# Which PSUM banks, which free places and which first products: one change to a two-layer decoder trunk in fp32

## The chip, the cores and the metric

The kernel runs on one core of a Trainium2 chip. The metric is device time in microseconds (us) of one execution; lower is better. The kernel before was timed in three runs: 577.90, 578.51 and 579.87 us, median 578.51.

## The reference

The input is x, 256 tokens by 1024, in float32. Two layers follow, each a token mixer and a gated MLP, and after each of these four parts x becomes LayerNorm(alpha * x + part).

- Layer 0 mixes with a gMLP: z = gelu(x @ w_in) (1024 by 2048) is halved into u and v, v is normalised, each of 8 groups of 128 channels is mixed over positions by a causal 128 by 128 matrix (once for each of two chunks of 128 tokens), a bias is added, and (u * mixed) @ w_out follows.
- Layer 1 mixes with attention: qkv = x @ w_qkv, 16 heads of 64. With 256 tokens there is one block, so it is plain causal attention with a relative position bias, and then @ w_o.
- The MLP: h = x @ w_up (1024 by 5632), a causal convolution of width 3 over tokens, gelu(g) * val, @ w_down (2816 by 1024).

## The kernel before

**Products in halves.** Every large product of fp32 matrices is made of three TensorE products of rounded parts: a matrix is split into `hi` (rounded to fp32r by ScalarE or VectorE) and `lo` (the rest, a VectorE subtraction, line 344), and hi*hi + hi*lo + lo*hi is summed in PSUM. `split` (line 357) records both instructions. All TensorE products of this kind have line 326 in the profile, all transposes line 332.

**Weights.** They come from HBM in 76 chunks of 1 MB in the order of `stream`. `prep(i)` (line 385) loads chunk i into one of two `raw` buffers and splits it into two pairs `whi`, `wlo` of 128 by 1024. Five chunks (`CHUNKS`) are prepared at the start; `spent` prepares chunk i + 5 when chunk i has been used. The first two chunks are loaded and split in pieces (`FIRST`, line 382). x comes transposed (`xT`) in four pieces (`XFIRST`), each split by `load_xt` (line 433), with its tiles in the order token half, k tile. The rank in these tables is the order of the loads on SP's queue. With two `raw` buffers, chunk 2 waits for the splits of chunk 0, chunk 3 for those of chunk 1.

**PSUM.** Eight banks (lines 271 to 316): four tiles of one bank each (`bank0` to `bank3`, the list `ALONE`), and two tiles of two banks each (`twos0`, `twos1`), whose halves can also be handed out one by one: banks 4 and 6 are the halves of `twos0`, 5 and 7 those of `twos1`, and `couple(j)` names such a pair. `bank()` hands out the oldest free single bank, or a half if all four are held long; `half()` a half of the tile that was used least recently; `taken(i, long)` a given one.

**Order.** Each helper records an operation with an estimated time in a plan. `Plan.emit` (line 122) walks through the plan with these estimates, gives every operation a due time from those that need it, and writes the instructions in the order of its own start times. TensorE's main products keep the recorded order; operations with `fill=True` (position mixing, scores, transposes, application of the attention weights) are put between them as soon as the plan finds them ready. On the chip each engine works through its instructions in that order, and waits where something is not ready. The plan knows of a PSUM half only by its own last user; the waits on the chip are put in by the framework from the accesses to the tiles in the written order.

**The stages.** `gmlp` (line 639): v by rows into four single banks (96 products of 512 columns, for k tiles 0 to 3 both token halves in turn, then each half alone); then eight groups of column products for u (`cols_times`, 24 products of 256 columns each, line 678: into a half), each read by ScalarE's gelu, with `spatial(g)` (line 667, also into a half) for the group three before. `project_out` (line 583) multiplies by w_out, w_down or w_o into four long held single banks and, for the last token half, two halves (`ends`), adds the residual and normalises. `conv_up` is the first half of the MLP. `moba` (line 758) is attention: V by rows into the four halves (line 771, token half 0 into couple 0), then for eight pairs of heads `project` (q, then k; line 787, into a half), `scores` (line 805, two single banks), `softmax`, `turn` (line 838, one single bank and three transposes for each head) and `apply` (line 849).

Of the kernel before, what the change touches and what calls it, by code (L numbers as in the profile page):

```python
# [11 lines left out]
F32 = mybir.dt.float32  # L12
# [6 lines left out]
P = 128  # L19
D = 1024  # L20
S = 256
DEPTH = 2
KT = D // P
FFN = 2816
FT = FFN // P
NT = S // P
# [9 lines left out]
HALF = 512  # L36
CH = 2048
# [8 lines left out]
T1_WAITS = (2600, 3300, 4000, 4700)  # L46
REST = 25000
AHEAD = 12000


class Buf:
# [172 lines left out]
def trunk_kernel(ctx: ExitStack, tc: tile.TileContext, a: dict, out: bass.AP):  # L224
# [64 lines left out]
    def couple(j):  # L289
        return j + BANKS // 2, j + BANKS // 2 + len(twos)  # L290
# [62 lines left out]
    def load(o, src, w, r=(), nbytes=None, rank=None):  # L353
        nbytes = nbytes or flat(o) * P * 4
        plan.op("sp", nbytes / 360.0, lambda: nc.sync.dma_start(o, src), r, w, nbytes=nbytes, rank=rank)  # L355
# [24 lines left out]


    FIRST = {0: [(0, 512, 0), (512, 1024, 2), (1024, 2048, 4)], 1: [(0, 1024, 6), (1024, 2048, 7)]}
    XFIRST = ((0, 1, 1), (1, 1, 3), (2, 2, 5), (4, 4, 8))

    def prep(i):
        name, c = stream[i]
        raw = raws.new()
        cuts = FIRST.get(i, [(0, CH, None)])
        for s, e, rank in cuts:
            load(raw.ap[:, s:e], a[name][c, :, s:e], [(raw, range(s // 256, e // 256))], rank=rank)  # L390
        subs = []
        for s in range(2):
            hi, lo = whi.new(), wlo.new()
            pieces = [(0, 512), (512, 1024)] if i in FIRST or i in FINE else [(0, SUB)]
            for b, e in pieces:
                src = raw.ap[:, s * SUB + b:s * SUB + e]
                split((hi, range(b // 256, e // 256), hi.ap[:, b:e]), (lo, range(b // 256, e // 256), lo.ap[:, b:e]),
                      (raw, range((s * SUB + b) // 256, (s * SUB + e) // 256), src))
            subs.append((hi, lo))
        chunks[i] = subs  # L400
# [5 lines left out]
    def sub(name, c, s):  # L406
        return chunks[where[name, c]][s]
# [18 lines left out]
    def xt_view(b):  # L426
        return b.ap

    xh, xl = xt_new()
    xT32 = place("ff", HALF, KT * S)  # L430
    xv32 = xT32.ap.rearrange("p (t k c) -> p t k c", t=NT, k=KT)

    def load_xt(k, n, rank):
        load(xv32[:, :, k:k + n, :], a["xT"][:, :, k:k + n, :], [(xT32, [(t, j) for t in range(NT) for j in range(k, k + n)])],
             rank=rank)
        for t in range(NT):
            parts = [(t, j) for j in range(k, k + n)]
            split((xh, parts, xt_view(xh)[:, t, k:k + n, :]), (xl, parts, xt_view(xl)[:, t, k:k + n, :]),
                  (xT32, parts, xv32[:, t, k:k + n, :]), by="dve" if k == 0 else "act")

    prep(0)
    for k, n, rank in XFIRST:
        load_xt(k, n, rank)
    for i in range(1, CHUNKS):
        prep(i)
    xtok = [Buf(t) for t in xs_]
# [192 lines left out]
    def gmlp():  # L639
        at = xt_at(xh, xl)  # L640
        pieces = [[(o, HALF, bank(True)) for o in (0, HALF)] for _ in range(NT)]
        order = [(k, t) for k in range(4) for t in range(NT)] + [(k, t) for t in range(NT) for k in range(4, KT)]
        v = []
        for k, t in order:
            rows_step(pieces[t], *at(k, t), *sub("a_v", k // 2, k % 2), k == 0, k == KT - 1)
            if t == NT - 1 and k % 2:
                spent("a_v", k // 2)
            if (k, t) == (3, NT - 1):
                rows = ln_rows(0)
                ws, bs = load_mixer()  # L650
            if k == KT - 1:
                vt = place("ff", HALF + t * D, D)
                for o, n, b in pieces[t]:
                    act(vt.ap[:, o:o + n], b.ap, AF.Gelu_apprx_tanh, [b], [(vt, range(o // S, (o + n) // S))],
                        psum=True, table="gelu")
                    done_with(b)
                st, mean, rstd = stats(vt, vt.ap, [(0, HALF), (HALF, HALF)])
                scaled(vt, vt.ap, st, mean, rstd, rows)
                v.append(vt)
        load_rest()  # L660
        mh, ml = place("rr", 0, KT * S), place("rr", KT * S, KT * S)
        hv, lv = (b.ap.rearrange("p (k s) -> p k s", k=KT) for b in (mh, ml))
        uring = Places("ff", [0, S, HALF + 2 * D, HALF + 2 * D + S], S)
        yring = Places("ff", range(5120, 6144, S), S)
        us = {}

        def spatial(g):
            b, y = half(), yring.new()
            mms([(b.ap[:, c * P:(c + 1) * P], v[c].ap[:, g * P:(g + 1) * P], ws[1][:, g, :], True, True)
                 for c in range(NT)], [(v[c], [g // 2]) for c in range(NT)] + [ws[0]], [b], fill=True)  # L670
            y3 = y.ap.rearrange("p (c t) -> p c t", c=NT)
            tt(y3, b.ap[:, :S].rearrange("p (c t) -> p c t", c=NT), bs[1][:, g:g + 1, :].to_broadcast([P, NT, P]),
               ALU.add, [b, bs[0]], [y])
            tt(y.ap, y.ap, us[g].ap, ALU.mult, [y, us[g]], [y])
            split((mh, [g], hv[:, g, :]), (ml, [g], lv[:, g, :]), (y, [0], y.ap))

        for g in range(GROUPS):
            b = half()
            cols_times(b, xh, xl, *sub("a_u", g // 2, g % 2))
            if g % 2:  # L680
                spent("a_u", g // 2)
            us[g] = uring.new()
            act(us[g].ap, b.ap[:, :S], AF.Gelu_apprx_tanh, [b], [us[g]], psum=True, table="gelu")
            if g >= 3:
                spatial(g - 3)
        for g in range(GROUPS - 3, GROUPS):
            plan.later(600 * (g - GROUPS + 4), lambda g=g: spatial(g))
        return lambda k, t: (hv[:, k, t * P:(t + 1) * P], lv[:, k, t * P:(t + 1) * P], [(mh, [k]), (ml, [k])])
# [69 lines left out]
    def moba(h, l, scr):  # L758
# [9 lines left out]
        ohv, olv = (b.ap.rearrange("p (k s) -> p k s", k=KT) for b in (oh, ol))  # L768
        vhv, vlv = (b.ap.rearrange("p (t d) -> p t d", t=NT) for b in (vh, vl))
        at = xt_at(h, l)  # L770
        pieces = [[(o, HALF, taken(i, True)) for o, i in zip((0, HALF), couple(j))] for j in range(NT)]
        for ks in (range(5), range(5, KT)):
            for t in range(NT):
                for k in ks:
# [10 lines left out]
        held, biases = {}, {}  # L785

        def project(i, j):
            b, t = half(), qkring[j].new()
            cols_times(b, h, l, *sub("b_qk", i, j))

            n, at2, scale = (P, P, DH ** -0.5) if j == 0 else (S, 0, 1.0)
            src, (th, tl) = b.ap[:, at2:at2 + n], (x.new() for x in qkparts[j])
            act(t.ap, b.ap[:, :P], AF.Copy, [b], [t], scale=scale, psum=True)
            act(th.ap, src, AF.Copy, [b], [th], scale=scale, psum=True)
            stt(tl.ap, src, scale, th.ap.bitcast(F32), ALU.mult, ALU.subtract, [b, th], [tl])
            t = (t, th, tl)
            held.setdefault(i, []).append(t)
            if j == 0:
                biases[i] = bring.new()
                load(biases[i].ap, bass.AP(tensor=scr.ap.tensor, offset=scr.ap.offset + 2 * i * DIST,  # L800
                                           ap=[[1, P], [DIST, 2], [1, S]]), [biases[i]], [scr])
            else:
                spent("b_qk", i)

        def scores(i):
            ((q0, qh, ql), (k0, kh, kl)), bias = held[i], biases[i]
            bank2 = [bank() for _ in range(2)]


            def both(o, seq):  # L810
                return [(bank2[hh].ap[:, o[0]:o[1]], x.ap[hh * DH:(hh + 1) * DH], y.ap[hh * DH:(hh + 1) * DH],
                         n == 0, n == len(seq) - 1) for n, (x, y) in enumerate(seq) for hh in range(2)]

            mms(both((0, P), [(q0, k0)]) + both((P, P + S), [(qh, kh), (qh, kl), (ql, kh)]),
                [q0, qh, ql, k0, kh, kl], bank2, fill=True)
            held[i] = [softmax(bank2[hh], bias, hh) for hh in range(2)]
# [20 lines left out]

        def turn(i):
            ph, pl = (x.new() for x in pring)
            for hh in range(2):  # L840
                e, b = held[i][hh], bank()

                transposes([(b.ap[:, c * P:(c + 1) * P], e.ap[:, c * P:(c + 1) * P]) for c in range(3)],
                           [(e, [0, 1])], [b])
                sl = slice(hh * (P + S), (hh + 1) * (P + S))
                split((ph, [hh], ph.ap[:, sl]), (pl, [hh], pl.ap[:, sl]), (b, [0], b.ap[:, :P + S]), psum=True)
            held[i] = ph, pl
# [57 lines left out]
def _layout(i):  # L905
# [10 lines left out]
    def paired(wa, wb):  # L916
# [3 lines left out]
    w_in, qkv = np.asarray(i["a_w_in"])[0], np.asarray(i["b_w_qkv"])[0]  # L920
    g = {
        "x": f(x.reshape(NT, P, D).transpose(1, 0, 2)),
        "xT": f(x.reshape(NT, P, KT, P).transpose(3, 0, 2, 1)),
        "a_v": by_rows(w_in[:, D:]),
        "a_u": f(tiles(w_in[:, :D]).reshape(4, 2, P, SUB).transpose(0, 2, 1, 3).reshape(4, P, CH)),
        "a_out": by_rows(np.asarray(i["a_w_out"])[0]),
# [45 lines left out]
```

## Time and profile before

| what | value |
|---|---|
| median of three runs | 578.51 us (577.90 to 579.87) |
| the profiled execution, its own time | 579.16 us |
| its span, first to last instruction | 577.5 us |
| TensorE (PE) busy | 560.1 us, 97% of the span |
| VectorE (DVE) busy | 473.7 us, 82% |
| ScalarE (ACT) busy | 361.9 us, 63% |
| share of PE in the chain that ended last | 92% |

The profile is of one execution. PE is TensorE's products, PEld its weight loads, DVE is VectorE, ACT ScalarE, SPq the queue of SyncE that issues the DMAs. In the timeline a row begins with the start in us and the busy time of the row, then engine, line, operation, output<-inputs, shapes and how often (x2: two merged). In brackets stands the engine's idle time before it and what released it. Products are pipelined and their ends are modelled, so what TensorE loses is read from the distance of two starts.

### The profile page before, as it was taken

What the parts mean: (1) busy time and instruction counts of PE and PEld (TensorE: products, weight loads), DVE (VectorE), ACT (ScalarE), POOL (GpSimd) and SP (SyncE); (2) the same over time, 40 slices, a digit from 0 to 9 for tenths busy, and PEclk for the clock granted to TensorE, in tenths of its full rate; (3) what the DMA queues carried; (4) which work ended last, traced back from release to release, by engine and by line L of the source; (5) the groups of instructions that cost most, each with busy time, mean ns of one, the idle gap of its engine ahead of it and who ended that gap; (6) DMA issues with size and microseconds to landing.
All of it is one profiled execution on the core that took longest, in us unless ns stands there. A gap on an engine that the chain in (4) does not pass through costs nothing.

```text
span 577.5 us, 8559 instructions
## 1 busy us (share of the span) xinstructions
PE 560.1 (97%) x3210; PEld 485.9 (84%) x3210; DVE 473.7 (82%) x885; ACT 361.9 (63%) x660; POOL 11.3 (2%) x17
## 2 busy tenths in 40 slices
PE   6998999999999999999999999999999999999994
PEld 4798888888888878888889998888888888888884
DVE  5587989999999997558878889879999999996426
ACT  5555567776677685435568777658777778785300
POOL 0020010000000000001000000000000000000001
PEclk9999999999999999999999999999999999999998
DMA  7887544537454567742663442515456555567202
GB/s 260 330 336 274 199 145 151 215 145 259 188 211 156 210 230 267 259 169 87 250 250 117 181 165 92 201 73 183 183 188 254 199 170 211 219 218 255 110 1 73
DMA packets 20133, 110.93 MB, mean 192 GB/s; under 512 B 2251, under 2 KB 6268, under 8 KB 7676
## 3 DMA queue, kind: packets, MB, share of 16 engines
q1 hardware_dynamic: 20092, 110.39, 53.0%
q8 instruction: 25, 0.41, 0.3%
q14 instruction: 16, 0.13, 0.1%
HBM read 109.31 MB, written 1.07 MB: 191 GB/s over the span
## 4 chain that ended last, share of the span: by engine, by line
PE 92%; DVE 3%; DMA 2%; ACT 2%; issue 0%; SPq 0%; DVEq 0%; ACTq 0%
PE twos L326 60%; PE bank L326 29%; DMA raw<-in_a_v 2%; PE bank L332 2%; DVE wlo L344 1%; DVE rr L344 1%; ACT ff L338 1%; DVE x L348 0%; ACT whi L338 0%; ACT rr L338 0%; SPq L355 0%; DVE ff L825 0%; PE twos L332 0%; DVE ff L834 0%; DVE stat L494 0%
## 5 line engine op out<-in xcount | busy, mean ns | idle before, releaser
L326 PE MATMUL twos<-xt,whi 128*128 128x512 f32 (+1 forms) x1024 | 295.1, 354 | 2.0 <-ACT ff L338 1.5
L344 DVE TENSOR_TENSOR wlo<-raw,whi 128x1024 fp32r<-128x1024 f32 (+1 forms) x212 | 228.4, 1098 | 30.8 <-ACT whi L338 30.3
L326 PE MATMUL twos<-xt,wlo 128*128 128x256 f32 x832 | 231.5, 278 | 0.0
L338 ACT ACTIVATE whi<-raw 128x1024 fp32r<-128x1024 f32 (+1 forms) x212 | 195.0, 954 | 56.7 <-DMA raw<-in_f_up 18.2
L326 PEld LDWEIGHTS twos<-xt,whi 128*128 128x128 f32 x1024 | 179.5, 189 | 31.7 <-ACT ff L338 2.4
L326 PEld LDWEIGHTS twos<-xt,wlo 128*128 128x128 f32 x832 | 156.8, 188 | 0.1
L326 PE MATMUL bank<-whi,rr 128*128 128x512 f32 x432 | 135.2, 391 | 0.4 <-DVE smax L825 0.4
L326 PEld LDWEIGHTS bank<-whi,rr 128*128 128x128 f32 x432 | 81.1, 188 | 18.0 <-issue 0.6
L326 PE MATMUL bank<-wlo,rr 128*128 128x512 f32 x216 | 84.1, 389 | 0.0
L348 DVE SCALAR_TENSOR_TENSOR ff<-ff,convc 128x255 f32<-128x255 f32 (+1 forms) x160 | 69.1, 477 | 0.0
L338 ACT ACTIVATE ff<-twos 128x512 f32<-128x512 f32 (+2 forms) x64 | 31.4, 491 | 53.4 <-PE twos L326 52.6
L326 PEld LDWEIGHTS bank<-wlo,rr 128*128 128x128 f32 x216 | 40.6, 188 | 8.1
L338 ACT ACTIVATE ff<-ff,convc 128x256 f32<-128x256 f32 x80 | 45.5, 592 | 2.9 <-DVE ff L344 2.5
L344 DVE TENSOR_TENSOR ff<-twos,ff 128x512 f32<-128x512 f32 (+1 forms) x48 | 30.9, 645 | 16.0 <-ACT ff L338 11.7
L326 PE MATMUL twos<-whi,xt 128*128 128x512 f32 x128 | 42.1, 396 | 0.5 <-DVE x L348 0.5
L338 ACT ACTIVATE ff<-bank,lncol 128x128 f32<-128x128 f32 x48 | 18.9, 460 | 29.1 <-PE bank L332 28.4
L348 DVE SCALAR_TENSOR_TENSOR x<-x,bank 128x512 f32<-128x512 f32 x16 | 11.0, 686 | 23.7 <-PE bank L326 23.6
L326 PEld LDWEIGHTS twos<-whi,xt 128*128 128x128 f32 x128 | 24.1, 188 | 5.7 <-DVE x L348 0.9
L326 PE MATMUL bank<-whi,xt 128*128 128x512 f32 x64 | 21.9, 420 | 5.1 <-DVE xt L361 5.0
L338 ACT ACTIVATE rr<-ff 128x256 fp32r<-128x256 f32 x52 | 21.0, 406 | 7.4 <-DVE ff L344 7.4
L326 PE MATMUL twos<-wlo,xt 128*128 128x512 f32 x64 | 25.0, 390 | 0.0
L344 DVE TENSOR_TENSOR ff<-ff 128x256 f32<-128x256 f32 x52 | 21.6, 418 | 0.5 <-ACT ff L338 0.2
(67 smaller groups left out, 416.9 us busy)
## 6 DMA issues: line engine op xcount, KB each, us to landing
raw<-in_f_up SPq DMA_DIRECT2D x44, 1024.0 KB, 4.8
raw<-in_f_dn SPq DMA_DIRECT2D x22, 1024.0 KB, 4.8
raw<-in_b_qk SPq DMA_DIRECT2D x8, 1024.0 KB, 4.8
lnrow<-in_lnrow SPq DMA_DIRECT2D x5, 1024.0 KB, 6.7
raw<-in_a_u SPq DMA_DIRECT2D x4, 1024.0 KB, 5.3
raw<-in_a_out SPq DMA_DIRECT2D x4, 1024.0 KB, 4.9
raw<-in_b_v SPq DMA_DIRECT2D x4, 1024.0 KB, 4.8
raw<-in_b_o SPq DMA_DIRECT2D x4, 1024.0 KB, 4.8
```

The costliest lines, as they stand in the source:

```text
L326: nc.tensor.matmul(o, l, x, start=start, stop=stop)
L332: nc.tensor.transpose(o, x, ident.ap)
L338: plan.op("act", ns, lambda: nc.scalar.activation(o, x, func, **kw), r, w, table=table)
L344: dve(70 + 1.04 * flat(x), lambda: nc.vector.tensor_tensor(o, x, y, op=op), r, w)
L348: lambda: nc.vector.scalar_tensor_tensor(o, x, s, y, op0=op0, op1=op1), r, w)
```

## The change

- `cols_times` for u (in `gmlp`) and for q and k (`project`) writes into `bank()` in place of `half()`.
- `scores` takes the two halves of `twos0`, `turn` those of `twos1`, and `turn` transposes both heads (six transposes) in one operation before the splits of either.
- V's token halves take the couples in the order of last use.
- `xT` lies in HBM and in SBUF by k tile, then token; `load_xt` splits two k tiles of both token halves in one instruction.
- Chunk 2 is loaded into a free place of `ff`, chunk 3 into the buffer of the LayerNorm rows (`rowring`); chunk 4 takes the first `raw` buffer, then free of chunk 0. The row load `ln_rows(0)`, and two loads for the mixer that overlap the place in `ff`, come behind the splits of these chunks.
- Eight products of zeros (128 by 128 by 512 columns) into a single bank are recorded ahead of everything, after a VectorE memset.
- The first k tile of V in `gmlp` is done in another order (`first_step`): for each half of the columns, hi*hi for both token halves, then lo*hi, then hi*lo.

```diff
+WARM = 8
...
+    EARLY = {2: lambda: place("ff", HALF + KT * S, CH), 3: rowring.new}
...
-        raw = raws.new()
+        raw = EARLY.get(i, raws.new)()
...
+        load(xT32.ap[:, sl], a["xT"][:, sl], [(xT32, parts)], rank=rank)
+        for j in range(k, k + n, 2):
+            m = min(2, k + n - j)
+            sl, parts = cut(j, m)
+            hv, lv = (both[:, j:j + m, o:o + S] for o in (0, S))
+            xv = xT32.ap[:, sl].rearrange("p (k x) -> p k x", k=m)
+            split((xh, parts, hv), (xl, parts, lv), (xT32, parts, xv), by="dve" if k == 0 else "act")
+    zeros, idle = place("rr", 0, HALF), bank()
+    dve(480, lambda: nc.vector.memset(zeros.ap.bitcast(F32), 0.0), (), [zeros])
+    for _ in range(WARM):
+        mms([(idle.ap, zeros.ap[:, :P], zeros.ap, True, True)], [zeros], [idle], fill=True)
...
+        def first_step():
+            (hi, lo), x = sub("a_v", 0, 0), [at(0, t) for t in range(NT)]
+            for p in range(2):
+                for part, w in ((0, hi), (1, hi), (0, lo)):
+                    for t in range(NT):
+                        o, n, b = pieces[t][p]
+                        mms([(b.ap, x[t][part], w.ap[:, o:o + n], part == 0 and w is hi, False)],
+                            x[t][2][part:part + 1] + [(w, range(o // 256, (o + n) // 256))], [b])
+            plan.tick()
...
         for g in range(GROUPS):
-            b = half()
+            b = bank()
             cols_times(b, xh, xl, *sub("a_u", g // 2, g % 2))
...
-        pieces = [[(o, HALF, taken(i, True)) for o, i in zip((0, HALF), couple(j))] for j in range(NT)]
+        free_first = sorted(range(NT), key=lambda j: max(bank_of[i][0] for i in couple(j)))
+        pieces = [[(o, HALF, taken(i, True)) for o, i in zip((0, HALF), couple(j))] for j in free_first]
...
-            b, t = half(), qkring[j].new()
+            b, t = bank(), qkring[j].new()
...
-            bank2 = [bank() for _ in range(2)]
+            bank2 = [taken(x, False) for x in couple(0)]
...
-            for hh in range(2):
-                e, b = held[i][hh], bank()
-                transposes([(b.ap[:, c * P:(c + 1) * P], e.ap[:, c * P:(c + 1) * P]) for c in range(3)],
-                           [(e, [0, 1])], [b])
+            bs = [taken(x, False) for x in couple(1)]
+            transposes([(b.ap[:, c * P:(c + 1) * P], e.ap[:, c * P:(c + 1) * P])
+                        for e, b in zip(held[i], bs) for c in range(3)], [(e, [0, 1]) for e in held[i]], bs)
+            for hh, b in enumerate(bs):
...
-        "xT": f(x.reshape(NT, P, KT, P).transpose(3, 0, 2, 1)),
+        "xT": f(x.reshape(NT, P, KT, P).transpose(3, 2, 0, 1).reshape(P, KT * S)),
```

## Rows read from the trace of the kernel before

**Rows 1.** Page, part 1, and waits of PE: us in total, times, longest.

```profile
PE 560.1 (97%) x3210; PEld 485.9 (84%) x3210; DVE 473.7 (82%) x885; ACT 361.9 (63%) x660; POOL 11.3 (2%) x17
...
PE twos L326 <- ACT ff L338: 1.5, 3, 0.5
```

**Rows 2.** Timeline of the first 24 us: start, busy us, engine, line, operation.

```profile
4.99 0.76 PE L326 MATMUL bank<-whi,xt 128*128 128x512 f32 x1 [4.99 <-DVE xt L361]
...
5.09 0.68 DVE L344 TENSOR_TENSOR wlo<-raw,whi 128x512 fp32r<-128x512 f32 x1
...
8.97 1.15 ACT L338 ACTIVATE whi<-raw 128x512 fp32r<-128x512 f32 x2 [0.76 <-DMA raw<-in_a_v]
...
9.63 1.29 DVE L344 TENSOR_TENSOR wlo<-raw,whi 128x512 fp32r<-128x512 f32 x2 [1.09 <-ACT whi L338]
...
10.26 0.63 PE L326 MATMUL bank<-whi,xt 128*128 128x512 f32 x2
...
10.72 0.40 PE L326 MATMUL bank<-wlo,xt 128*128 128x512 f32 x1
...
10.96 3.60 SPq L355 DMA_DIRECT2D raw<-in_a_v  x2
...
17.85 2.00 ACT L338 ACTIVATE whi<-raw 128x1024 fp32r<-128x1024 f32 x2 [3.20 <-DMA raw<-in_a_v]
...
18.45 1.01 PE L326 MATMUL bank<-whi,xt 128*128 128x512 f32 x2
...
18.95 2.36 DVE L344 TENSOR_TENSOR wlo<-raw,whi 128x1024 fp32r<-128x1024 f32 x2 [3.49 <-ACT whi L338]
...
20.23 0.50 PE L326 MATMUL bank<-wlo,xt 128*128 128x512 f32 x1 [0.77 <-DVE wlo L344]
```

**Rows 3.** Busy time by window: stretch, length, PE, PEld, DVE, ACT, POOL, clock, DMA share, GB/s.

```profile
8.00:12.00 4.00, 4.00 (x14) 3.12 (x14) 2.85 (x7) 3.03 (x8) 0.00 (x0) 1.00 1.02 394
...
15.00:16.00 1.00, 1.00 (x6) 0.81 (x6) 0.45 (x1) 0.00 (x0) 0.00 (x0) 1.00 1.09 213
```

**Rows 4.** Timeline, column products for u, 43 to 54 us.

```profile
43.92 0.28 PE L326 MATMUL twos<-xt,wlo 128*128 128x256 f32 x1
...
44.24 0.38 ACT L338 ACTIVATE ff<-twos 128x256 f32<-128x256 f32 x1 [2.83 <-PE twos L326]
...
44.68 0.50 PE L326 MATMUL twos<-xt,whi 128*128 128x256 f32 x2 [0.47 <-ACT ff L338]
...
45.02 0.28 PE L326 MATMUL twos<-xt,wlo 128*128 128x256 f32 x1
...
52.55 0.61 PE L326 MATMUL twos<-ff 128*128 128x128 f32 x4
...
53.25 0.39 PE L326 MATMUL twos<-xt,whi 128*128 128x256 f32 x1
```

**Rows 5.** Timeline, start of attention's V, 269 to 271 us.

```profile
269.54 0.39 PE L326 MATMUL twos<-whi,xt 128*128 128x512 f32 x1
...
269.96 0.42 DVE L348 SCALAR_TENSOR_TENSOR x<-x,twos 128x256 f32<-128x256 f32 x1
...
270.44 0.50 PE L326 MATMUL twos<-whi,xt 128*128 128x512 f32 x1 [0.51 <-DVE x L348]
```

**Rows 6.** Timeline, splits of V and the second projection, 290 to 297 us.

```profile
290.32 0.60 ACT L338 ACTIVATE rr<-twos 128x512 fp32r<-128x512 f32 x1 [0.76 <-DVE rr L344]
...
290.96 0.69 DVE L344 TENSOR_TENSOR rr<-twos,rr 128x512 fp32r<-128x512 f32 x1 [0.67 <-ACT rr L338]
...
295.60 0.28 PE L326 MATMUL twos<-xt,wlo 128*128 128x256 f32 x1
296.28 0.50 PE L326 MATMUL twos<-xt,whi 128*128 128x256 f32 x2 [0.40 <-DVE rr L344]
```

**Rows 7.** Timeline, last scores and start of the product by w_o.

```profile
358.01 0.49 PE L326 MATMUL bank<-ff 64*128 64x128 f32 x4 [0.57 <-ACT ff L338]
...
358.95 0.50 PE L326 MATMUL bank<-qk,qk 64*128 64x256 f32 x4 [0.33 <-DVE qk L348]
...
361.10 0.51 PE L326 MATMUL bank<-whi,rr 128*128 128x512 f32 x1 [0.40 <-DVE smax L825]
```

**Rows 8.** Busy time by window, four pairs of heads; columns as in rows 3.

```profile
317.05:350.39 33.34, 33.34 (x279) 31.74 (x279) 29.14 (x97) 24.55 (x73) 0.00 (x0) 1.00 0.42 151
```

More of the change, by code (lines that the diff above doesn't have):

```diff
@@ L430, in trunk_kernel, with cut @@
     xT32 = place("ff", HALF, KT * S)
-    xv32 = xT32.ap.rearrange("p (t k c) -> p t k c", t=NT, k=KT)
     def load_xt(k, n, rank):
[L434 to L439, printed above, removed]
+        def cut(j, m):
+            return slice(j * S, (j + m) * S), [(t, i) for t in range(NT) for i in range(j, j + m)]
+        sl, parts = cut(k, n)
+        load(xT32.ap[:, sl], a["xT"][:, sl], [(xT32, parts)], rank=rank)
[9 more added lines that the diff above has]
+        mms([(idle.ap, zeros.ap[:, :P], zeros.ap, True, True)], [zeros], [idle], fill=True)
     prep(0)
-    for k, n, rank in XFIRST:
-        load_xt(k, n, rank)
+    for x in XFIRST:
+        load_xt(*x)
     for i in range(1, CHUNKS):
@@ L643, in gmlp @@
         v = []
+        def first_step():
[7 more added lines that the diff above has]
+            plan.tick()
         for k, t in order:
+            if k == 0:
+                if t == 0:
+                    first_step()
+                continue
             rows_step(pieces[t], *at(k, t), *sub("a_v", k // 2, k % 2), k == 0, k == KT - 1)
```

## The prediction

> **What bounds the kernel now.** I read the page first: TensorE is busy 97% of the span [rows 1]. So a change that leaves its products alone can win only what TensorE loses between them. Then the waits of PE: they name few and short ones. I looked these up in the timeline and read the loss from start to start, because a busy row hides part of a wait: where the view of waits counts 0.47 us, TensorE's starts are 0.76 apart instead of 0.12 [rows 4]. Three kinds of place remain. At the start, weights come late. In the column products for u, four waits are for a reader of PSUM. Around attention there are waits at V's first products, at the second projection and at the last scores. The end of the kernel, behind the last product, is not touched.
>
> **The start.** The first product runs at 4.99, released by the split of x. Twelve products (k tile 0) fill the 5.27 us to 10.26, about 0.44 each; from there two take 0.46 us, 0.23 each [rows 2]. That is the distance of the two clock levels, 1.2 and 2.4 GHz. It looks like 2.5 us to be had from eight zero products that raise the clock earlier. It is not. K tile 1 needs the second half of chunk 0: its `hi` begins at 8.97, its two `lo` run from 9.63 to 10.92. With a full clock k tile 0 would be done near 8, and TensorE would wait. After the last `lo` at 10.92 some eight products of tile 1 are left, 8 * 0.23, so tile 1 ends at about 12.8; before it ends at 10.26 + 12 * 0.23 = 13.0. I take 0.2 us. `first_step` and the larger x pieces work on k tile 0 too, ahead of the same late half chunk: nothing more. The zeros cost nothing while they end before 4.99: the memset lies between 0.06 us (the smallest VectorE row) and the 0.68 of a 128x512 subtraction [rows 2], so it ends between 1.0 and 1.6; eight products at 0.44 are 3.5 us, so they end between 4.5 and 5.1. At worst the first product is 0.1 late, and k tile 0 has more than that to spare. On VectorE the memset delays nothing: its first work, the split of x, is done just before 4.99.
>
> Behind that comes chunk 2. Its `hi` begins at 17.85, when its load has landed, its `lo` at 18.95; TensorE issues two products at 18.45 and the next at 20.23: 1.78 less 0.46 is 1.3 us lost [rows 2]. Chunk 2 was issued at 10.96, after chunk 0's splits, and chunk 3 about 3.3 us behind it. Now both are queued right after x, near 6.5. Does that bring them sooner? From 8 to 12 the DMA engines are full, share 1.02 at 394 GB/s: an earlier issue gains nothing there. But from 15 to 16 the share is 1.09 at only 213 GB/s [rows 3], in the second after chunk 3's late issue, and chunk 2 lands after that. With both queued I expect that dip to go, and chunk 2 to land near 16. Its `lo` is then ready near 18.2, and TensorE arrives at about 18.5. Gain 1.3, with chunk 3's smaller wait 1.4; bounds 0 (it lands at 17.8 again) and 2.4 (the half chunk too comes a microsecond sooner). I take the upper of the likely values because the dip stands where the late issue is. The row load and the two mixer loads that now queue behind the splits of chunks 2 and 3 are wanted by VectorE only for the mixing, not by a product of v: free. Start in all: 0.2 + 1.4 = **1.6**.
>
> **u.** The product after 43.92 starts at 44.68, after a gelu at 44.24 [rows 4]. That gelu reads the group just finished, in the other half of the same two-bank tile: from group 3 on, `half()` gives every u group a half of `twos1`, and the spatials `twos0`. So the wait is one between two banks of one tile. It costs 0.76 - 0.12, and the restart 0.34 for two products instead of 0.24: 0.74 in all. Three such waits [rows 1] make 2.2; a fourth, behind a spatial, 0.70 for four short products that fill about half of it, 0.3. With four single banks a group's bank comes round after four groups, over 11 us. Who is late next? The w_out product takes the banks of the last four groups: the gelu of group 7 has three pieces (2 us) before its bank is written. The weights come as fast as before, five chunks ahead. Gain **2.5**, bounds 1.9 and 2.5.
>
> Row and rule differ here. The Trainium skill, page "PSUM — Partial Sum Buffer", section "PSUM bank collisions raise a hardware error", lets engines work at the same time in different banks and asks for a guard by bank and quadrant. By that rule these waits would not exist and the sum would be 3.1 less, with those of the second projection.
>
> **Attention.** V's second piece waits from 269.54 to 270.44, 0.90 less 0.23, for the residual add of the piece that ended last, in the same tile [rows 5]; the add itself had to wait for V's first piece. The older couple first: **0.7**. The second projection waits for V's last split, 0.68 less 0.12 [rows 6]; in a single bank: **0.6**.
>
> At the end, scores wait 0.57 and 0.33 us for the last k, and w_o waits 0.40 for the softmax to read a score bank [rows 7]: 1.3, more by starts. Now w_o has banks that were free long ago and can run while k is read. Not all of that stays. `apply` of pair 6 takes a half of `twos0`, which the last scores hold until both heads are read, and `apply` of pair 7 is wanted at the same time as before with the product around it earlier. Bounds -0.7 and 1.3, I take **0.6**, nearer the rows that go.
>
> In the loop, `turn` reads two halves of one tile. The splits of V do that now, and ScalarE and VectorE wait for each other, 0.76 and 0.67 [rows 6]. In `turn` both halves are ready together, so ScalarE can read both, then VectorE both; VectorE then waits one ScalarE read longer, some 0.3 us by half of 0.67. VectorE is busy 29.14 of 33.34 us in four pairs [rows 8], 1.05 idle per pair, which takes that up: **-0.2**, bounds 0 and -2.5. Six transposes in one operation take what two times three take.
>
> **Sum.** 1.6 + 2.5 + 0.7 + 0.6 + 0.6 - 0.2 = 5.8 us. The profiled execution, 579.16 us, becomes 573.4. It stands 0.65 above the median, 578.51; from the median: **572.7 us**. A difference under 0.3% (1.7 us) can't be told from no change.
>
> **Rivals.**
> - *Chunk 2 comes no sooner.* The bytes ahead of it are the same, and the engines are full until 12 [rows 3]. Then 1.4 goes: 574.1. Against it: the dip after 15. Chance 0.22.
> - *The end of attention gives back.* `apply` waits in `twos0` and the chain of pair 7 ends late: 0.6 becomes -0.7, and the loop costs another 0.7: 574.7. Chance 0.15.
> - *The waits are not of the tiles*, as the rule would have it: 575.8. Against it: the release at 44.68 comes right after a read of another bank [rows 4]. Chance 0.04.
> - *Slower: VectorE becomes the bound of the attention loop.* If `turn` makes the two engines wait in turns as V's splits do, a pair holds VectorE up by 0.76 + 0.67 = 1.4. With half of its 1.05 idle taking that up, 0.9 * 8 = 7.2 instead of 0.2: 579.7; with none, 11.4 and 584. It decides from 0.75 per pair on, where the whole gain is lost. For it: VectorE's 87% [rows 8]. Against it: both halves are ready at once, which V's are not. Chance 0.07.
>
> My forecast has 0.52. The range: both bounds of the start, and the two rivals at 574 to 575, lie within **569.9 to 576.0**; at the low end everything at its better bound, 2.6 + 2.5 + 0.7 + 0.6 + 1.3 = 7.7, and a bit for waits that I left out. Faster 0.87 (the forecast, the first three rivals and little else), within 0.3% 0.07, slower 0.06.
>
> **What would show it.** In the profile after: no wait of PE for a gelu in the u products, their starts 0.12 apart; eight products from about 1.5 us on, and products of k tile 0 at 0.23 each from about 7; then a wait before the first product of k tile 1, which still follows its late half chunk; chunk 2's `hi` near 16 in place of 17.85; the first product for u 1.6 us earlier and the first by w_out about 4 us earlier than before. V's first products without a wait. In the loop, pairs still 8.3 to 8.4 us apart and VectorE under 95%. The prediction is wrong if chunk 2's `hi` stays at 17.8, if a pair takes over 9 us, or if the clock falls back while TensorE waits for k tile 1: products at 0.44 after 10 us would each cost 0.2.

## The result and the profile after

The changed kernel takes 573.84 us (median of six runs, 573.69 to 574.93), the kernel before, beside it on the same chips, 578.93 (577.9 to 580.26): ratio 0.9914, 95% interval 0.9898 to 0.9931. That is 5.1 us less, inside the range of the forecast (569.9 to 576.0) and 1.1 us above its 572.7. The profiled execution took 573.73 us, span 572.0, against 579.16 and 577.5.

The page, part 1, then the waits of PE (us in total, times, longest), to be read beside [rows 1]:

```profile
PE 560.6 (98%) x3218; PEld 486.8 (85%) x3218; DVE 473.6 (83%) x882; ACT 362.3 (63%) x658; POOL 10.0 (2%) x17
...
PE bank L327 <- ACT whi L339: 1.9, 1, 1.9
PE bank L327 <- DVE nhalf L425: 1.5, 1, 1.5
PE bank L327 <- DVE wlo L345: 0.2, 1, 0.2
```

Three waits are left, all in the first 20 us; the 1.5 is only the stretch ahead of the zero products. Those for a gelu, for the residual add, for V's split and for the softmax's read are gone. The span can be cut at the same products in both traces, and the differences of the stretches add up to what the whole span lost:

| stretch, between the first or last products named | before, us | after, us | difference | forecast |
|---|---|---|---|---|
| start, to v's last product | 31.06 | 30.40 | -0.66 | -1.6 |
| u and the product by w_out | 46.92 | 44.47 | -2.45 | -2.5 |
| feed-forward, up to V's first product | 191.09 | 191.09 | 0 | 0 |
| V | 23.55 | 22.65 | -0.90 | -0.7 |
| projections and loop over pairs | 64.04 | 63.51 | -0.53 | -0.6 + 0.2 |
| end of attention, product by w_o | 23.83 | 22.83 | -1.00 | -0.6 |
| the rest | 196.96 | 197.04 | +0.08 | 0 |
| sum | 577.45 | 571.99 | -5.46 | -5.8 |

So one row is off by much, the start. Its timeline, beside [rows 2]:

```profile
0.98 0.48 DVE L451 MEMSET rr<- 128x512 f32 x1 [0.98 <-PEq L996]
...
1.52 3.78 PE L327 MATMUL bank<-rr 128*128 128x512 f32 x8 [1.52 <-DVE nhalf L425]
...
7.22 1.07 PE L327 MATMUL bank<-whi,xt 128*128 128x512 f32 x4
...
8.13 0.61 PE L327 MATMUL bank<-wlo,xt 128*128 128x512 f32 x2
...
9.91 1.15 ACT L339 ACTIVATE whi<-raw 128x512 fp32r<-128x512 f32 x2 [3.64 <-DMA raw<-in_a_v]
...
10.60 0.49 PE L327 MATMUL bank<-whi,xt 128*128 128x512 f32 x1 [1.85 <-ACT whi L339]
...
17.46 2.01 ACT L339 ACTIVATE whi<-ff 128x1024 fp32r<-128x1024 f32 x2 [1.34 <-DMA ff<-in_a_v]
...
19.84 0.50 PE L327 MATMUL bank<-wlo,xt 128*128 128x512 f32 x1
```

The zero products do what they are for: k tile 0's products start 0.23 us apart from 7.22 on, and its last one starts at 8.35 instead of 10.26. Then TensorE stands for 1.85 us, because the second half of chunk 0 is split at 9.91, nearly a microsecond later than before (8.97). And chunk 2's split begins at 17.46, where 16 was forecast.

Busy time by window, columns as in [rows 3]:

```profile
8.00:12.00 4.00, 1.92 (x8) 1.03 (x7) 1.43 (x3) 1.78 (x3) 0.00 (x0) 1.00 0.94 358
...
15.00:16.00 1.00, 1.00 (x6) 0.84 (x5) 1.00 (x3) 1.00 (x2) 0.00 (x0) 1.00 0.97 410
```

The dip to 213 GB/s is gone, as forecast, and chunk 2 is late all the same.

The places that went as forecast, in the timeline: u's products [rows 4], V's first and the second projection's first product [rows 5, 6], w_o ahead of the last scores [rows 7].

```profile
49.71 0.28 PE L327 MATMUL bank<-xt,wlo 128*128 128x256 f32 x1
49.83 0.40 PE L327 MATMUL bank<-xt,whi 128*128 128x256 f32 x2
50.07 0.28 PE L327 MATMUL bank<-xt,wlo 128*128 128x256 f32 x1
...
265.84 0.28 PE L327 MATMUL twos<-whi,rr 128*128 128x256 f32 x1
265.96 0.40 PE L327 MATMUL twos<-whi,xt 128*128 128x512 f32 x1
266.19 0.40 PE L327 MATMUL twos<-wlo,xt 128*128 128x512 f32 x1
...
288.61 0.39 PE L327 MATMUL twos<-whi,xt 128*128 128x512 f32 x1
288.83 0.40 PE L327 MATMUL bank<-xt,whi 128*128 128x256 f32 x2
...
352.94 0.48 PE L327 MATMUL bank<-whi,rr 128*128 128x512 f32 x1
...
354.51 0.49 PE L327 MATMUL twos<-ff 64*128 64x128 f32 x4
```

Each product starts as soon as the one before it allows: 0.12 us apart for 256 columns, 0.23 for 512. Four pairs of heads, beside [rows 8]:

```profile
304.29:337.00 32.71, 32.71 (x271) 30.84 (x270) 30.00 (x102) 27.29 (x76) 0.00 (x0) 1.00 0.52 176
```

A pair takes 32.71 / 4 = 8.18 us, VectorE is busy 92%, and TensorE waits nowhere in the loop.

### The profile page after: what moved, and what is told of

Its sections match the earlier page's. It is cut to its first block, busy times and chain, and to the rows that moved or that the text cites. A ratio compares the mean times of both kernels' runs of the same rounds, so it can differ in the third digit from the quotient of the medians.

```text
span 572.0 us, 8564 instructions
## 1 busy us (share of the span) xinstructions
PE 560.6 (98%) x3218; PEld 486.8 (85%) x3218; DVE 473.6 (83%) x882; ACT 362.3 (63%) x658; POOL 10.0 (2%) x17
## 3 DMA queue, kind: packets, MB, share of 16 engines
HBM read 109.31 MB, written 1.07 MB: 193 GB/s over the span
## 4 chain that ended last, share of the span: by engine, by line
PE 94%; DVE 2%; DMA 1%; ACT 1%; issue 0%; SPq 0%; DVEq 0%; ACTq 0%
PE twos L327 52%; PE bank L327 41%; DMA raw<-in_a_v 1%; PE bank L333 1%; PE twos L333 1%; DVE x L349 0%; ACT ff L339 0%; DVE wlo L345 0%; DVE rr L345 0%; DVE ff L856 0%; SPq L356 0%; ACT rr L339 0%; ACT whi L339 0%; ACT qk L339 0%; DVE stat L508 0%
## 5 line engine op out<-in xcount | busy, mean ns | idle before, releaser
L327 PE MATMUL twos<-xt,whi 128*128 128x512 f32 x640 | 222.2, 394 | 0.0
L327 PE MATMUL twos<-xt,wlo 128*128 128x256 f32 x640 | 177.3, 277 | 0.0
L327 PEld LDWEIGHTS twos<-xt,whi 128*128 128x128 f32 x640 | 120.0, 188 | 27.8
L327 PEld LDWEIGHTS twos<-xt,wlo 128*128 128x128 f32 x640 | 120.1, 188 | 0.1
L349 DVE SCALAR_TENSOR_TENSOR ff<-ff,convc 128x254 f32<-128x254 f32 (+1 forms) x160 | 69.9, 478 | 2.9 <-ACT ff L339 2.5
L327 PE MATMUL bank<-xt,whi 128*128 128x256 f32 x384 | 71.3, 286 | 0.0
L327 PEld LDWEIGHTS bank<-xt,whi 128*128 128x128 f32 x384 | 59.7, 191 | 0.8
L327 PE MATMUL bank<-xt,wlo 128*128 128x256 f32 x192 | 54.3, 283 | 0.0
L339 ACT ACTIVATE ff<-twos 128x512 f32<-128x512 f32 x40 | 23.9, 596 | 40.4 <-PE twos L327 40.3
L327 PEld LDWEIGHTS bank<-xt,wlo 128*128 128x128 f32 x192 | 36.7, 191 | 0.0
```

The source lines that it names most:

```text
L327: nc.tensor.matmul(o, l, x, start=start, stop=stop)
L339: plan.op("act", ns, lambda: nc.scalar.activation(o, x, func, **kw), r, w, table=table)
L349: lambda: nc.vector.scalar_tensor_tensor(o, x, s, y, op0=op0, op1=op1), r, w)
```

## The experiments: one part undone, one part alone

No part of the computation is left out in any of these but the eight zero products, in no_zeros and xh_no_zeros. Times stand against the kernel before on the same chip.

**u_half: the changed kernel, u's groups back in halves of the two-bank tiles.**

```diff
-            b = bank()
+            b = half()
             cols_times(b, xh, xl, *sub("a_u", g // 2, g % 2))
```

> The changed kernel with the eight u groups of the gMLP back in halves of the two-bank tiles; all else as changed. Theory (a reader of the other half of the tile holds the next group up): the four waits come back, 2.5 us slower than the changed kernel, a time near 576.3 us, ratio to before near 0.9957; in the profile PE waits for a gelu again with starts 0.7 to 0.8 us apart. Rival (different banks need no wait, the gain of 2.45 us in that stretch came from the earlier weights): within 0.4 us of the changed kernel, 573.8.

Measured: 578.58 us, ratio 0.9997 (0.9986 to 1.0009). The waits of PE that come back:

```profile
PE twos L327 <- ACT ff L339: 2.1, 4, 0.5
...
PE twos L327 <- DVE ff L345: 0.5, 1, 0.5
```

The waits are those of the tile, then: with the halves they are there, with single banks they aren't. There are five of them instead of the four of before; u and w_out take 48.22 us, 3.75 more than in the changed kernel and 1.3 more than in the kernel before. Undoing this one line costs 4.7 us by the medians, nearly the whole gain; but the 1.3 us stand with a wait that the kernel before did not have, so they are not what the line won.

**att_before: the changed kernel, the four edits of attention undone** (V's couples by number, second projection in a half, scores and turns in single banks).

```diff
-for j in free_first]
+for j in range(NT)]
...
-            b, t = bank(), qkring[j].new()
+            b, t = half(), qkring[j].new()
...
-            bank2 = [taken(x, False) for x in couple(0)]
+            bank2 = [bank() for _ in range(2)]
```

(and `turn` as in the kernel before)

> The changed kernel with all four edits in attention undone (V's tiles in fixed order, projections in halves, scores and turns in single banks). Theory: the waits at V's start, at the second projection and at the last scores come back, 2.4 us slower than the changed kernel, 576.2 us, of that 0.9 at V, 0.5 up to the last projection, 1.0 at the product by w_o. Rival (part of the 2.4 comes from VectorE and ScalarE having been delayed less by earlier stages): 1 to 1.5 us slower.

Measured: 574.13 us (0.9925, 0.9902 to 0.9948), 0.3 from the changed kernel and less than either expectation. In its trace V takes 23.55 us again (+0.90), the loop 63.30 (-0.2), the end of attention 22.91 (+0.1). So in this order of work only V's edit earns something. The medians show less than 0.9, and the six runs are wide apart (572.06 to 576.56). Its profiled execution shows one reason: the granted clock, in the column before the last two.

```profile
12.00:16.00 4.00, 4.00 (x12) 3.17 (x11) 3.48 (x6) 3.34 (x6) 0.00 (x0) 0.57 1.02 430
13.00:16.00 3.00, 3.00 (x8) 2.33 (x8) 2.92 (x5) 2.76 (x6) 0.00 (x0) 0.50 1.03 433
```

From 13 to 16 us the granted clock is 0.50, the lower of the two levels (1.2 GHz), and products start 0.43 apart. Before that TensorE had stood for 2.17 us, waiting for the half chunk, and worked again from 10.68. v ends at 31.75 instead of 30.40.

**late_chunks: chunks 2 and 3 loaded as before the change.**

```diff
-    EARLY = {2: lambda: place("ff", HALF + KT * S, CH), 3: rowring.new}
+    EARLY = {}
```

> The changed kernel with chunks 2 and 3 in the two raw buffers again, so that they are issued after the splits of chunks 0 and 1. Theory A (the late issue makes the dip of the DMA rate after 15 us): chunk 2's split starts near 18.5, later than the 17.46 of the changed kernel, and TensorE loses about 1 us more: 574.8. Theory B (the bytes in front set the landing): chunk 2 lands as before within 0.3 us and the time is that of the changed kernel, 573.8 +- 0.3. In both the half chunk of k tile 1 should land as it did, at 9 to 10 us.

Measured: 574.37 us (0.9925, 0.9908 to 0.9942), 0.5 more than the changed kernel, which its six runs (572.80 to 575.28) do not show by themselves; v ends at 30.92 instead of 30.40. Chunk 2's split begins at 17.58:

```profile
17.58 2.01 ACT L339 ACTIVATE whi<-raw 128x1024 fp32r<-128x1024 f32 x2 [1.31 <-DMA raw<-in_a_v]
```

Issuing chunk 2 at 6.87 instead of 12.30, then, moved its landing by 0.1 us in these two executions; what the early places save is the wait for chunk 3 that follows.

**no_zeros: the changed kernel without the zero products** (the memset and the bank stay).

```diff
-WARM = 8
+WARM = 0
```

> The changed kernel without the eight products of zeros (their memset and bank stay). Theory (k tile 1 waits for its half chunk whatever the clock): the twelve products of k tile 0 take 0.43 us each and end near 10.2, the half chunk's split comes at 9.9 to 10.5, and the time is within 0.3 us of the changed kernel. Rival (the clock is worth its full price): 2.5 us slower, 576.3. Between them: the wait for k tile 1 leaves TensorE short of work, so the clock rises only after 12 us, and 10 to 15 products run at 0.43 instead of 0.23: 2 to 3 us slower too, but with the loss behind 10 us and not ahead of it.

Measured: 573.80 us (0.9916, 0.9901 to 0.9932): no difference. K tile 0 is then done near 9.9, k tile 1 starts at 10.85 after the same half chunk. The zeros are worth nothing here.

**Each part alone on the kernel before.** only_u:

```diff
-            b = half()
+            b = bank()
             cols_times(b, xh, xl, *sub("a_u", g // 2, g % 2))
```

> The kernel before with the u groups in single banks alone. Theory A (what it saves is the waits of that stretch): 2.5 us less than before, 576.3, and attention's waits stay where they were. Theory B (a new order reaches attention too): attention's stretch from V's end to the end of w_o shrinks by 1 us or more besides, 575.0. Rival to both (the parts do not add, since undoing it cost 4.1 us in the profiled run): 574.5.

only_att, the diff of att_before the other way round, on the kernel before:

```diff
-for j in range(NT)]
+for j in free_first]
...
-            b, t = half(), qkring[j].new()
+            b, t = bank(), qkring[j].new()
...
-            bank2 = [bank() for _ in range(2)]
+            bank2 = [taken(x, False) for x in couple(0)]
```

> The kernel before with the four attention edits alone (V's tiles by last use, projections in single banks, scores and turns in the two-bank tiles). Undoing the four in the changed kernel cost only about 0.8 us of its span, of which 0.9 at V's start; yet the changed kernel gained 2.4 us in that stretch over the one before. Theory A (the edits are worth 2.4 in the order of the kernel before, where they meet the waits at the second projection and the last scores): 576.4. Theory B (only V's start is theirs, the rest comes from another order of the instructions that the earlier edits bring about): 577.9.

only_start, all of the change's first three hunks with `first_step`:

```diff
+    EARLY = {2: lambda: place("ff", HALF + KT * S, CH), 3: rowring.new}
...
+    for _ in range(WARM):
+        mms([(idle.ap, zeros.ap[:, :P], zeros.ap, True, True)], [zeros], [idle], fill=True)
...
+            if k == 0:
+                if t == 0:
+                    first_step()
+                continue
```

> The kernel before with the edits of the start alone (zeros, x by k tile, early chunks 2 and 3, the first step of v). Theory A (the start gains 0.7 us and nothing follows): 578.1. Theory B (the earlier start makes a fifth wait in the u groups, as in the run with u in halves, and gives the gain back): 578.5 to 579.5, five waits of PE for a gelu or a spatial's reader in the u groups instead of four.

| part | alone: us | ratio | undone in the changed kernel |
|---|---|---|---|
| u | 575.25 | 0.9945 (0.9927 to 0.9963) | +4.7 |
| attention | 576.32 | 0.9955 (0.9938 to 0.9972) | +0.3 |
| start | 578.63 | 1.0000 (0.9985 to 1.0016) | `EARLY` +0.5, zeros 0 |

Against the 578.40 of these runs the parts alone give 3.15, 2.08 and -0.23, each with an interval of about 1 us either way, which adds up to 5.0, nearly the 5.1 of the whole; undone one at a time they give other numbers. The order that the plan writes has a part in this. The start edits shift it: in only_start, u and w_out take 48.24 us, as in u_half, with a fifth wait for a half, while attention, untouched there, gets shorter: the loop by 0.72 (63.32), its end by 0.91 (22.92). In only_att, in the order of before, the edits themselves win at the end of attention: 1.49, and V 1.07; the loop stays at 64.05, though the wait at the second projection is gone from the list. So the end of attention can be had by either, and not twice. With u alone the waits of attention stand as before:

```profile
PE twos L326 <- DVE x L348: 0.5, 1, 0.5
PE bank L326 <- DVE smax L825: 0.4, 1, 0.4
PE twos L326 <- DVE rr L344: 0.4, 1, 0.4
```

only_start's profiled execution has the fallen clock too (0.57 from 12 to 16, 0.50 from 13), and v ends at 31.74. `first_step` and the row loads that were moved have no run of their own.

## The experiments: why the start gave so little

**x_halves: the changed kernel, x in the layout of before** (by halves of 128 rows, not by k tile; `load_xt` as it was).

```diff
-        "xT": f(x.reshape(NT, P, KT, P).transpose(3, 2, 0, 1).reshape(P, KT * S)),
+        "xT": f(x.reshape(NT, P, KT, P).transpose(3, 0, 2, 1)),
```

> The changed kernel with x in its old layout (token half, then k tile; two splits for each piece). The second half of chunk 0, which k tile 1 needs, landed at 8.95 us in the kernel before and at 9.9 to 10.3 in the profiles of the five kernels with x by k tile. Theory A (the layout does it): it lands near 9.0 again, k tile 1 begins a microsecond sooner, and chunk 2 then decides: 573.2. Theory B (landing there is set by the shorter issues behind it, or by chance): 9.9 to 10.3, and 573.8 to 574.3.

Measured: 572.18 us (572.01 to 572.54), 0.9889 (0.9872 to 0.9906), better than both kernels. TensorE's products stand in the order of the changed kernel, and 1.41 of the 1.57 us that the span gets shorter lie ahead of v's end:

```profile
8.73 1.15 ACT L339 ACTIVATE whi<-raw 128x512 fp32r<-128x512 f32 x2 [0.78 <-DMA raw<-in_a_v]
...
9.41 0.50 PE L327 MATMUL bank<-whi,xt 128*128 128x512 f32 x1 [1.00 <-ACT whi L339]
...
16.05 2.01 ACT L339 ACTIVATE whi<-ff 128x1024 fp32r<-128x1024 f32 x2 [1.32 <-DMA ff<-in_a_v]
```

Chunk 2 lands near 16, as forecast, and v ends at 28.99, 2.07 before the kernel before. So x's layout, which I had costed at nothing, held back the start. Chance in the landing is an unlikely reason: chunk 2's split begins at 17.45 to 17.69 in the six profiled executions with x by k tile in the changed kernel's order of loads, and at 15.72 to 16.08 in the three with x by halves and early chunks. Four more runs look for how.

**x_small: x by k tile, in smaller pieces.**

```diff
-    XFIRST = ((0, 1, 1), (1, 1, 3), (2, 2, 5), (4, 4, 8))
+    XFIRST = ((0, 1, 1), (1, 1, 3), (2, 1, 5), (3, 1, 6), (4, 2, 9), (6, 2, 10))
```

(chunk 1's ranks 6 and 7 become 7 and 8)

> The changed kernel, x still by k tile, but its last two loads cut in two: pieces of 1, 1, 1, 1, 2, 2 k tiles, so that a line of a load is as short as in the layout by halves (1 KB and 2 KB in place of 2 KB and 4 KB). Theory T (a load's share of the DMA engines goes by the length of its lines: the longer lines of x take the turn from the half chunk that was issued before them): the half chunk's split begins at 8.7 to 9.1 in place of 9.91, k tile 1 at 9.4 to 9.8, the last product of v near 29.3, time 572.3 to 573.0. Rival Q (SyncE issues the x loads in 0.42 us in place of 0.55 to 0.65, so what is behind the half chunk is in the queues sooner, whatever its lines): here issues are as quick and two more, the split stays at 9.8 to 10.2, time 573.6 to 574.2.

Measured: 573.11 us (573.0 to 573.15), 0.9895 (0.9869 to 0.9921).

```profile
8.47 1.15 ACT L339 ACTIVATE whi<-raw 128x512 fp32r<-128x512 f32 x2 [2.25 <-DMA raw<-in_a_v]
...
9.16 0.50 PE L327 MATMUL bank<-whi,xt 128*128 128x512 f32 x1 [0.16 <-ACT whi L339]
...
17.05 2.01 ACT L339 ACTIVATE whi<-ff 128x1024 fp32r<-128x1024 f32 x2 [1.64 <-DMA ff<-in_a_v]
```

The half chunk comes 1.44 us sooner, with issues as quick as before: rival Q falls. But v ends only 0.41 sooner, at 29.99, for chunk 2 is next: it comes 0.41 sooner. The time lies just above theory T's range (572.3 to 573.0), its v well behind the 29.3 that T gave.

**half_sooner: the half chunk issued ahead of x's k tile 1.**

```diff
-FIRST = {0: [(0, 512, 0), (512, 1024, 2), (1024, 2048, 4)], ...
-XFIRST = ((0, 1, 1), (1, 1, 3), ...
+FIRST = {0: [(0, 512, 0), (512, 1024, 2), (1024, 2048, 3)], ...
+XFIRST = ((0, 1, 1), (1, 1, 4), ...
```

> The changed kernel with chunk 0's second half issued ahead of x's k tile 1 in place of behind it. K tile 1 needs both, so this only moves about 128 KB and one issue of 0.43 us from before the half chunk to behind it. If what is issued behind it is what delays it (theories T and Q alike), the split comes by the one issue sooner: 9.4 to 9.6, and x tile 1 is still in time, since it was there at 5.87: 573.3 to 573.6, hardly to be told from the changed kernel's 573.84. If the order of issue is what counts, the 128 KB are worth 0.4 us more at 300 GB/s: the split near 9.0, 572.9.

Measured: 571.88 us (571.62 to 572.7), 0.9874 (0.9844 to 0.9903).

```profile
7.22 0.63 ACT L339 ACTIVATE whi<-raw 128x512 fp32r<-128x512 f32 x1 [1.33 <-DMA raw<-in_a_v]
...
8.65 0.39 PE L327 MATMUL bank<-whi,xt 128*128 128x512 f32 x1
...
16.14 2.01 ACT L339 ACTIVATE whi<-ff 128x1024 fp32r<-128x1024 f32 x2 [1.33 <-DMA ff<-in_a_v]
```

One swap of two loads brings the half chunk 2.7 us sooner, far more than either expectation, and TensorE passes from k tile 0 to 1 without a wait.

**xh_sooner: x by halves and that swap.**

```diff
+FIRST = {0: [(0, 512, 0), (512, 1024, 2), (1024, 2048, 3)], ...
+XFIRST = ((0, 1, 1), (1, 1, 4), ...
...
+        "xT": f(x.reshape(NT, P, KT, P).transpose(3, 0, 2, 1)),
```

> The kernel with x by halves, with chunk 0's second half issued ahead of x's k tile 1. There x tile 1 was split at 7.44 and the half chunk at 8.73, and k tile 1 began at 9.41, so the half chunk still comes last. It should come 0.3 to 0.6 us sooner, x tile 1 later by as much. ScalarE's splits then follow one on another up to chunk 2, which lands near 16: a gain of 0 to 0.4 us, 571.8 to 572.2. Rival: the split of x tile 1 comes late (after 8.7) and k tile 1 waits for that: 572.2 to 572.8.

Measured: 572.21 us (571.45 to 572.57), 0.9877 (0.985 to 0.9904). Its profiled execution is the shortest, span 570.0, chunk 2 at 15.72, v's end at 28.65; by the medians x_halves, half_sooner and this one can't be told apart.

**xh_no_zeros: x by halves, no zero products.**

```diff
-WARM = 8
+WARM = 0
...
+        "xT": f(x.reshape(NT, P, KT, P).transpose(3, 0, 2, 1)),
```

> The kernel with x by halves, without the eight zero products. With x by k tile they were worth nothing (573.80 without them, 573.84 with them), since k tile 1 waited for the half chunk to 10.60 with either. With x by halves k tile 1 begins at 9.41. Without the zeros k tile 0's twelve products take 0.43 to 0.44 us each up to about 10.2, as before the change. Theory A: the 0.8 us are then lost to the end: 572.8 to 573.1. Rival: chunk 2, whose split begins at 16.05, ends the wait in v for either, and the plan's order around the start differs a little: 572.0 to 572.4.

Measured: 572.02 us (571.9 to 572.52), 0.9878 (0.9852 to 0.9905): no difference to x_halves, the rival's case.

```profile
7.66 1.50 PE L327 MATMUL bank<-whi,xt 128*128 128x512 f32 x4
...
9.46 0.40 PE L327 MATMUL bank<-whi,xt 128*128 128x512 f32 x1
...
16.08 2.01 ACT L339 ACTIVATE whi<-ff 128x1024 fp32r<-128x1024 f32 x2 [1.33 <-DMA ff<-in_a_v]
```

Without the zeros the products come closer together from about 8 us on, and k tile 1 starts at 9.46 instead of 9.41.

Two regularities come out of the start in all of them. The first: v's last product stands 12.93 to 12.98 us behind the start of chunk 2's split in all eight profiled executions of kernels that load it early and in which the clock held. Chunk 2 fixes the end of v there; zeros, `first_step` and k tile 1 come before it, and what they win or lose is made up for by its wait. That wait is short, though: by the distances of starts TensorE loses about 0.3 us at chunk 2's first products in the changed kernel and 0.1 in x_halves, so chunk 2 alone, sooner by more than that, would have won no more. In the four executions that load late (before, only_u, only_att, late_chunks) it is chunk 3 that fixes it: v's last product stands 10.21 to 10.26 us behind the start of chunk 3's split. The second is in the semaphore events of the trace: a load lands in 16 parts, as many as there are DMA engines. When the first and the last part landed, and the mean:

```
               half chunk 0             chunk 2                v's last product
               first  mean  last        first  mean   last
before         6.96   7.65  8.95        15.42  16.04  17.83    31.06
after          6.64   7.83  9.89        13.92  15.50  17.44    30.40
no_zeros       6.88   8.15  10.14       13.98  15.69  17.67    30.62
x_small        6.14   7.17  8.45        14.22  15.47  17.03    29.99
x_halves       6.92   7.68  8.71        14.97  15.42  16.02    28.99
half_sooner    5.40   6.22  7.20        14.28  14.93  16.12    29.08
late_chunks    6.86   8.21  10.30       16.64  16.95  17.55    30.92
only_att       6.81   7.74  8.87        15.32  15.56  15.94    30.86
```

Chunk 2's mean is the same in the changed kernel and in x_halves (15.50, 15.42). What differs is the spread: 3.52 us against 1.05. On average the parts come as soon, but with x by k tile some of them fall some 2 us behind between 5 and 9 us, at the half chunk, and the lag stays from load to load, as if each engine worked through its parts in order. A load counts when its last part is there (chunk 2's at 17.44, its split at 17.46). In late_chunks, where the DMA share from 12 to 16 us is 0.88 in place of 1.02, the lag is gone by chunk 2: its parts land within 0.91 us of each other, though on average 1.45 later than in the changed kernel. Theory T came near x_small's half chunk (8.47, forecast 8.7 to 9.1), but its mechanism is not what the parts show: x's next load did not take the turn, its parts land behind those of the half chunk (first 7.27 after 6.64, last 11.11 after 9.89). What throws the engines out of step there, and why shorter pieces and the swap lessen it, stays open. I see only that single packets stall: between 2 and 5 us the changed kernel has six packets of 4 KB that take 0.98 us on average, where those from 12 to 16 us take 0.16. And the longest packet of the first 12 us takes 1.33 to 1.87 us in the six executions with x by k tile and the changed order of loads, 0.71 to 1.27 in the eight others.

## Why the prediction was right, and where it was off

- **u, 2.5:** 2.45, and 2.64 with u alone (44.28). The mechanism is shown by u_half and by the waits that left the list: with halves of a two-bank tile five waits and 48.22 us, with single banks none and 44.47. They hang on the tile that the program names, which holds two banks. The rival that they are not of the tiles falls. By the rule of the Trainium skill, page "PSUM — Partial Sum Buffer", section "PSUM bank collisions raise a hardware error", engines may work in different banks at once, and a guard between the two halves would not be needed; the measured waits decide here.
- **V, 0.7:** 0.90, and 0.90 again when undone. **Second projection less the loop, 0.4:** 0.53 in the profile after, but not shown to be the edits': undone in the changed kernel the stretch is 0.2 shorter still (63.30), and with the edits alone it is what it was (64.05). **End of attention, 0.6:** 1.00, but not for my reason alone: only_start gets 0.91 there by another order, without the edits. `apply` of pair 6 did not have to give back what w_o won; that rival (574.7) falls.
- **Slower by VectorE in the loop:** a pair takes 8.18 us with VectorE at 92%. It falls.
- **The zeros, 0.2:** nothing, in either layout. That k tile 0 ends early and then waits was right, and the reason why they give nothing reaches further: chunk 2 decides. The reckoning had a slip: at 10.26 k tile 0's last product starts, and k tile 1 follows at 10.49, so it should have given 0.4 in place of 0.2.
- **The start, 1.6: measured 0.66. This is the step that failed,** and in it the sentence that the larger x pieces do "nothing more". They brought x sooner and the last part of the half chunk 0.94 us later, and chunk 2 to 17.46 in place of 16. By the distances of TensorE's starts, k tile 1 begins 0.1 later than before (10.60 against 10.49) where I had 0.2 gained, 0.7 more is lost from there to chunk 2's first products, and 1.4 less behind these. So the waits at chunks 2 and 3 did shrink by the 1.4 of the forecast, but 0.8 of it only because TensorE came to chunk 2 that much later; chunk 2 itself came 0.4 sooner. The term for k tiles 0 and 1, 0.2, had become a loss of 0.8. With x by halves the start gives 2.07, within my bounds, chunk 2 at 16.05.
- The reasoning from the dip does not come out. In only_att, which loads late, the rate falls to 172 GB/s from 15 to 16 us, and chunk 2 lands as soon as in x_halves all the same; chunk 3 is what comes late, its split at 20.60 against 18.54 in x_halves:

```profile
15.96 2.01 ACT L338 ACTIVATE whi<-raw 128x1024 fp32r<-128x1024 f32 x2 [1.42 <-DMA raw<-in_a_v]
...
20.60 2.01 ACT L338 ACTIVATE whi<-raw 128x1024 fp32r<-128x1024 f32 x2 [2.63 <-DMA raw<-in_a_v]
```

- So the rival "chunk 2 comes no sooner" (574.1) came nearest to the time by luck: its 1.4 did not go, and what went was lost ahead of chunk 2. Its reason, that an early issue brings chunk 2 itself nothing, has only_att for it.
- I had also read chunk 2's 17.85 as a fixed property of the kernel before. The same start ran in only_att and only_u: 15.96 and 17.01, with v's end at 30.86 and 30.94, because chunk 3 is late next. Its 1.3 us were one execution's; for the end of v, chunk 2 and 3 had to come sooner together, which `EARLY` does.
- **"Wrong if the clock falls back":** not in the profiled execution after, but in those of att_before and only_start, at about the forecast's price: 1.35 us of v. In the changed kernel's runs, two of six have a lower mean granted clock (0.993 and 0.992 against 0.995 and 0.996) and are the longest, 574.33 and 574.93; and the two profiled executions in which it fell have 0.993 and 0.992 as well. That these are the same event is likely and not shown.

The sum was nearly right, then, since u and V were, for the reasons given, and by luck besides: a start that was overrated by 0.9 was partly made up by an end of attention that was underrated by 0.4.

## What to carry to other kernels

Look for waits of TensorE on a reader of the *other* half of a two-bank tile: giving each group of products a bank of its own was one line and worth most of this change. Before paying for an earlier start, find the load that sets the end of the stage, and look at the landing of its last part, not at issue times or mean rates; a layout that only serves an earlier piece of work can delay it. Where a change moves the planned order, test each part both alone and undone: the two prices can differ (attention here: 2.1 alone, 0.3 undone), and a part's gain may come from the order and not from the edit.

## What was not expected of the hardware

- Loads whose parts are out of step: one load's 16 parts land up to 3.9 us apart, with nearly the same mean for chunk 2 as without the lag (15.50 against 15.42), and the lag stays over five loads and more (half chunk 9.89 - 6.64 = 3.25, chunk 2 17.44 - 13.92 = 3.52).
- Swapping two loads, an issue 0.47 us earlier, moved the landing of a 512 KB load by 2.7 us (9.89 to 7.20).
- The granted clock fell to 0.50 for 3 us after a wait of 2.2 us in two profiled executions, and did not fall after one of 2.3 us in late_chunks' (1.00 from 11 to 20 us). The length of the wait alone doesn't tell it.
